# A Hymba decoder step: mixer norms on 32 partitions and as jobs between scan levels, sample states loaded two levels ahead, the last 264 tokens as two tiles of 128 and one of 8

## The chip, the core and the metric

The kernel runs on one NeuronCore of a Trainium2 chip. The metric is device time in microseconds (us), the median of several executions; lower is better. The core has five engines with their own instruction queues: PE (TensorE, matrix products), DVE (VectorE), ACT (ScalarE), POOL (GpSimd) and SP (SyncE, which here issues the DMAs).

## What is computed

One step of a hybrid decoder with one layer, in f32: 16 learned tokens and 1024 prompt tokens, which form one sequence, and 8 sample tokens, each with its own state; 1048 columns in all, model width 1024.

```python
h = h + 0.5 * swiglu(rmsnorm(h, n1), w1g, w1u, w1d)          # FFN 1, inner width 2816
u = rmsnorm(h, nm) @ w_in
q, fz, iv, g, z, xbc, dt_raw = jnp.split(u, SPLITS, axis=-1)
# HGRN2, 4 heads of 128: S_t = diag(f_t) S_{t-1} + k_t v_t^T, o_t = S_t^T q_t
o_hg = o_hg * lax.rsqrt(jnp.mean(o_hg * o_hg, axis=-1, keepdims=True) + EPS)   # per head
o_hg = o_hg.reshape(bsz, seqlen, HG_WIDTH) * hg_norm * jax.nn.silu(g)
# Mamba-2, 8 heads of 64, 2 groups, state 128, chunked scan; then
yz = (y * jax.nn.silu(z)).reshape(bsz, seqlen, SSM_GROUPS, -1)
yz = yz * lax.rsqrt(jnp.mean(yz * yz, axis=-1, keepdims=True) + EPS)           # per group of 256
h = h + jnp.concatenate([o_hg, yz], axis=-1) @ w_out
h = h + 0.5 * swiglu(rmsnorm(h, n2), w2g, w2u, w2d)          # FFN 2
y = rmsnorm(h, norm_final)
```

The prompt's results, the samples' results and the states of both kinds go out.

## The kernel before

Features lie on the 128 partitions and tokens along the free axis. Large products run at reduced operand precision with each operand split into a high and a low part, three matmuls for one (`mm3`, lines 163 to 165). The program has three stages: FFN 1, the mixer, and output projection with FFN 2 and the final norm.

In the FFNs the order on PE, DVE, ACT and SP is the program's own: a list of steps (`Steps`), each some matmuls of PE, with functions hung before a step by its number. In the mixer only PE's order is the program's; Tile's scheduler sets that of the other engines.

In the mixer the projections for q, f, v, g of each HGRN2 head and for z are a filler (`Fill`). One step of it, `fill(1)`, is one `mm3`, and `fill(n)` stands at every place where PE would wait for another engine. `fill.jobs` holds functions that run every so many fill steps; the Mamba-2 sample updates (`ssm_samples`) are such jobs.

The places the change touches:

- `ssm_scan`: nine chunks, eight of 128 tokens and one of 16. `back` makes the products with the old state (L1252), the causal block (L1257) and the new state (L1261).
- `hgrn_scan`: for each head a scan over levels m = 1, 2, 4, ... 64. A level has one batch of small products (L1540, or L1531 for m of 32 and more), then DVE multiplies q and k on (L1562, L1563), then `fill(5)`. `samples` loads four sample states and the samples' v rows, broadcast over the partitions, and updates them at once: four steps on ACT (L1488), four on DVE (L1489), then a store. It runs at m = 1 and m = 32. At the end the outputs are made in three pieces (L1619 to L1630); L1630 reads a sample's state with its q column, one column for each product.
- `hgrn_out` and `ssm_norm`: sums of squares over the partitions by a product with a matrix of ones (L1648, L1396), which puts the sum on all 128 partitions, then x to the power -1/2 by Ln, Exp and one Newton step (`rstd_wide`, L187) on 128 x 1032. `hgrn_out` returns five jobs, of which one runs after each level of the next head's scan; `ssm_norm` runs in one piece, that of group 0 ahead of head 1's scan.
- The final norm, on tokens: `Final` transposes 128 tokens (8 products), squares and sums on ACT, takes the root, and scales with `norm_final` on DVE. `LastFinal` does the last 264 of FFN 2's columns, three tiles of 88, in three parts, so that what is complete early is transposed early. They hang before steps of the last group of down products, whose results DVE adds to h (L763).

## Time and profile before

| | us |
|---|---|
| three executions | 1979.84, 1977.38, 1979.36 |
| median | 1979.36 |
| profiled execution | 1983.28 |
| its span | 1981.5 |
| PE busy in the span | 1937.6 |
| DVE, ACT, POOL busy | 1455.1, 835.4, 85.7 |

FFN 1 ends near 760 us, the mixer near 1190. A row of the windows view gives for a stretch of time its length, the busy time of the engines asked for (with instructions in brackets), the clock granted to TensorE as a share of full speed, the DMA engines' mean busy share and the GB/s moved. A row of the chain of waits gives start, length and work; a row of the timeline also shapes and, in square brackets, the idle time before it and what ended that. PEld is PE's weight loading.

### The profile page before, as it was taken

To read this page: it belongs to the slowest core of one execution; us is meant where nothing else is said; L and a number is where in the kernel's file an instruction comes from. 1 tells how busy PE (TensorE), PEld (TensorE's weight loads), DVE (VectorE), ACT (ScalarE), POOL (GpSimd) and SP (SyncE) were. 2 spreads that over 40 slices of the span, in tenths; PEclk is the share of its full clock that TensorE was granted. 3 is DMA by queue.
4 is the path that set the end of the run, shared out by engine and by line. 5 is a ranking of instruction groups with operands and counts; after the bars stand their busy time and mean duration, and the time that the engine had idled before them with its cause. 6 is when DMAs were issued, how large, how long until landed. Compare 5 with 4: busy or idle time off the path is not lost.

```text
span 1981.5 us, 40896 instructions
## 1 busy us (share of the span) xinstructions
PE 1937.6 (98%) x16687; PEld 1900.4 (96%) x16687; DVE 1455.1 (73%) x2515; ACT 835.4 (42%) x1587; POOL 85.7 (4%) x135
## 2 busy tenths in 40 slices
PE   7999999999999999999999999999999999999997
PEld 6999999999999999998989999999999999999997
DVE  7777777778688776575665567987777777768974
ACT  7522222224534655465544445742222222354352
POOL 4000000000000410000000002200000000000000
PEclk9999999999999999999999999999999999999999
DMA  7233242335976542232442254224232423487851
GB/s 219 78 100 98 82 129 82 112 83 155 295 246 223 175 133 60 55 102 63 131 121 67 78 167 141 71 87 117 85 109 81 127 83 113 152 245 237 270 179 67
DMA packets 323876, 258.45 MB, mean 130 GB/s; under 512 B 17568, under 2 KB 299424, under 8 KB 323680
## 3 DMA queue, kind: packets, MB, share of 16 engines
q1 hardware_dynamic: 323448, 255.79, 42.6%
q8 instruction: 132, 2.16, 0.5%
q14 instruction: 56, 0.46, 0.1%
q0 software_dynamic: 224, 0.04, 0.0%
q10 hardware_dynamic: 16, 0.00, 0.0%
HBM read 190.79 MB, written 65.05 MB: 129 GB/s over the span
## 4 chain that ended last, share of the span: by engine, by line
PE 84%; DVE 9%; DMA 2%; issue 2%; ACT 2%; SPq 0%; POOL 0%; DVEq 0%; ACTq 0%; POOLq 0%
PE acc L163 26%; PE acc L165 26%; PE acc L164 26%; DVE u L354 1%; DVE ws L468 1%; PE mis L1540 1%; DMA r<-in_w_ffn_up_dram 1%; DMA u<-hd 1%; DVE u L677 1%; DVE ws L739 1%; DVE u L343 0%; PE mis L1261 0%; DVE r L460 0%; PE mis L1600 0%; DVE t L548 0%
## 5 line engine op out<-in xcount | busy, mean ns | idle before, releaser
L163 PE MATMUL acc<-u,ws 128*128 128x258 f32 (+4 forms) x4482 | 1310.8, 293 | 8.4 <-DVE t L562 2.7
L164 PE MATMUL acc<-u,ws 128*128 128x258 f32 (+4 forms) x4482 | 1300.4, 290 | 3.3 <-DVE u L354 1.8
L165 PE MATMUL acc<-u,ws 128*128 128x258 f32 (+4 forms) x4482 | 1297.5, 290 | 3.4 <-DVE ws L468 3.3
L163 PEld LDWEIGHTS acc<-u,ws 128*128 128x128 f32 x4482 | 849.2, 190 | 13.6 <-issue 5.1
L164 PEld LDWEIGHTS acc<-u,ws 128*128 128x128 f32 x4482 | 851.6, 190 | 6.1 <-DVE u L354 2.8
L165 PEld LDWEIGHTS acc<-u,ws 128*128 128x128 f32 x4482 | 849.0, 189 | 5.3 <-DVE ws L468 4.9
L468 DVE TENSOR_TENSOR ws<-r,ws 128x512 fp32r<-128x512 f32 x308 | 212.8, 692 | 78.8 <-ACT ws L464 78.8
L464 ACT CAST ws<-r 128x512 fp32r<-128x512 f32 x308 | 173.8, 615 | 5.0 <-DVE r L460 4.8
L583 ACT ACTIVATE t<-t 128x524 f32<-128x524 f32 (+1 forms) x47 | 29.9, 640 | 299.6 <-DVE t L548 299.6
L460 DVE TENSOR_TENSOR r<-r,r 128x512 f32<-128x512 f32 x176 | 121.1, 690 | 8.3 <-DMA r<-in_w_ffn_up_dram 6.5
L560 ACT ACTIVATE t<-t 128x516 f32<-128x516 f32 (+1 forms) x41 | 26.2, 639 | 200.3 <-DVE t L548 200.3
L677 DVE TENSOR_TENSOR u<-u,u 128x1048 fp32r<-128x1048 f32 (+3 forms) x84 | 97.2, 1159 | 10.2 <-ACT u L673 9.4
L232 POOL TENSOR_TENSOR t<-t,t 128x262 f32<-128x262 f32 (+1 forms) x56 | 57.5, 1036 | 814.9 <-ACT t L231 811.8
L548 DVE TENSOR_TENSOR t<-t,u 128x524 f32<-128x524 f32 (+1 forms) x135 | 90.4, 698 | 2.8
L158 DVE TENSOR_TENSOR ws<-r,ws 128x512 fp32r<-128x512 f32 x88 | 60.9, 702 | 40.0 <-ACT ws L157 39.5
L734 ACT CAST ws<-u 128x512 fp32r<-128x512 f32 (+1 forms) x72 | 42.1, 585 | 99.9 <-DVE u L729 91.6
L673 ACT CAST u<-u 128x1048 fp32r<-128x1048 f32 (+3 forms) x84 | 82.8, 988 | 1.3 <-DMA u<-hd 1.3
L763 DVE SCALAR_TENSOR_TENSOR s<-acc,s 128x524 f32<-128x524 f32 (+3 forms) x86 | 53.8, 649 | 33.8 <-PE acc L165 33.5
L739 DVE TENSOR_TENSOR ws<-r,ws 128x512 fp32r<-128x512 f32 (+1 forms) x84 | 56.3, 681 | 29.8 <-ACT ws L734 29.5
L734 ACT CAST ws<-r 128x512 fp32r<-128x512 f32 (+1 forms) x84 | 47.5, 582 | 65.9 <-DVE r L729 39.7
L553 ACT COPY t<-acc 128x524 f32<-128x524 f32 (+3 forms) x46 | 26.4, 574 | 103.5 <-PE acc L165 103.5
L157 ACT CAST ws<-r 128x512 fp32r<-128x512 f32 x88 | 53.6, 617 | 34.5 <-PE acc L165 31.1
(393 smaller groups left out, 1875.2 us busy)
## 6 DMA issues: line engine op xcount, KB each, us to landing
r<-in_w_ffn_down_dram SPq DMA_DIRECT2D x128, 256.0 KB
hd<-s SPq DMA_DIRECT2D x93, 258.0 KB
r<-in_w_ffn_gate_dram SPq DMA_DIRECT2D x88, 256.0 KB
r<-in_w_ffn_up_dram SPq DMA_DIRECT2D x88, 256.0 KB
hd<-s SPq DMA_DIRECT2D x77, 262.0 KB
u<-hd SPq DMA_DIRECT2D x36, 516.0 KB
u<-hd SPq DMA_DIRECT2D x28, 524.0 KB
r<-in_w_in_dram SPq DMA_DIRECT2D x56, 256.0 KB
```

What stands on the lines that cost most here:

```text
L158: self.nc.vector.tensor_sub(lo, src, hi.bitcast(F32))
L163: mm(ps, whi, xhi, start=first, stop=False, skip_group_check=more)
L164: mm(ps, whi, xlo, start=False, stop=False, skip_group_check=more)
L165: mm(ps, wlo, xhi, start=False, stop=last, skip_group_check=more)
L460: self.K.nc.vector.tensor_tensor(self.raw[p], self.raw[x], self.raw[y], op)
L464: self.K.nc.scalar.copy(self.w[p][:, : self.n * P], self.raw[p])
L468: self.K.nc.vector.tensor_sub(t[:, 512 : 512 + w], self.raw[p], t[:, :w].bitcast(F32))
L548: nc.vector.tensor_mul(t, t if src is None else src, spread.lanes(i, cs))
L673: K.nc.scalar.copy(hi, lo.bitcast(F32))
L677: K.nc.vector.tensor_sub(lo, lo.bitcast(F32), hi.bitcast(F32))
L734: nc.scalar.copy(w[p, j, g][:, : n * P], src)
L739: nc.vector.tensor_sub(t[:, 512 : 512 + n * P], box[0], t[:, : n * P].bitcast(F32))
```

## The change

The norms of the mixer use a new class `Rms`. `root` makes four products whose weights are 32 columns of ones, so that the sums of the four quarters of the 1032 columns land on four strips of 32 partitions, 258 columns wide; Ln, Exp and (in `newton`, two jobs later) the Newton step run on that. `part(i)` spreads a quarter over 128 partitions by a product with one row of ones. `hgrn_out` multiplies the gate with the product's result in PSUM; `ssm_norm` copies it to SBUF, and returns seven jobs. Those of group 0 run after the levels of head 1's scan.

`samples` is parted: `samples_load` at m = 1 and m = 8, the update at m = 4 and m = 64. The samples' outputs are made from the other side: q column by q column padded to 32 columns of weights, the state as the moving operand, four results to a bank on strips of 32 partitions; the rows are copied and then turned by two transposes of four columns each.

In the 16-token chunk two `fill(2)` stand between the three products. `LastFinal` has tiles of 128, 128 and 8; a product of its first part goes from DVE to POOL, its squares of the second part become one instruction instead of two, and the three `Final` at the end stand at other steps, one with other banks.

```diff
+class Rms:
...
+    def root(self):
+        K, w = self.K, self.w
+        nc = K.nc
+        ps = K.psm()[:, :w]
+        for i in range(4):
+            nc.tensor.matmul(ps[32 * i : 32 * i + 32], K.ones[1][:, :32], self.v[:, i * w : i * w + w], start=True, stop=True)
+        self.r, self.q = K.t(w), K.t(w)
+        an = nc.scalar.activation(self.q, ps, AF.Identity, scale=self.scale, bias=K.eps)
+        with K.tc.issue_after(an.ins):
+            ld = nc.scalar.preload_act_table_set("natural_log_exp_and_others")
+        with K.tc.issue_after(ld.ins):
+            nc.scalar.activation(self.r, self.q, AF.Ln)
+            nc.scalar.activation(self.r, self.r, AF.Exp, scale=-0.5, bias=K.lna)
+    def newton(self):
...
+    def part(self, i):
+        K, w = self.K, self.w
+        ps = K.psm()[:, :w]
+        K.nc.tensor.matmul(ps, K.ones[1][32 * i : 32 * i + 1], self.r[32 * i : 32 * i + 1], start=True, stop=True)
+        return ps, slice(i * w, i * w + w)
...
+        if n < P:
+            fill(2)
         py = K.psm()
...
+        if n < P:
+            fill(2)
         ps = K.psm()
...
-def ssm_norm(K, g, tag, fill):
+def ssm_norm(K, g, tag, then):
...
+    return [rms.root, lambda: None, rms.newton, lambda: (spread(0), spread(1)), lambda: (spread(2), spread(3)), lambda: scale(0, ya), end]
...
-        if m in (1, 32):
-            samples({1: 0, 32: 4}[m])
+        if m in (1, 8):
+            samples_load({1: 0, 8: 4}[m])
         if jobs:
             jobs.pop(0)()
             fill(2)
+        if m in (4, 64):
+            samples({4: 0, 64: 4}[m])
         fill(5)
...
+    qz = K.t(32 * NS).rearrange("p (b i) -> p b i", b=NS)
+    nc.gpsimd.memset(qz, 0.0)
+    nc.scalar.copy(qz[:, :, 0], qs[:, :NS])
     fill(6)
+    pr = K.psm()
+    for b in range(NS):
+        nc.tensor.matmul(pr[32 * (b % 4) : 32 * (b % 4) + 32, b // 4 * P : b // 4 * P + P], qz[:, b], states[b // 4 * 4][:, b % 4], start=True, stop=True)
+    rows = K.t(2 * P)
+    nc.scalar.copy(rows, pr[:, : 2 * P])
+    fill(1)
...
-    for b in range(NS):
-        nc.tensor.matmul(po8[:, 16 + b : 17 + b], states[b // 4 * 4][:, b % 4], qs[:, b : b + 1], start=True, stop=True)
+    for i in range(2):
+        nc.tensor.matmul(po8[:, 16 + 4 * i : 20 + 4 * i], rows[:, i * P : i * P + P], K.ident[:, 0:P:32], start=True, stop=True)
...
-    jobs = [root, None, None, None, gate]
-    return [lambda i=i: jobs[i]() for i in range(5)]
+    return [rms.root, lambda: None, rms.newton, lambda: (gate(0), gate(1)), lambda: (gate(2), end())]
...
-            self.part(j, ps, 0, 4, 0)
+            K.nc.scalar.activation(yt[:n, 512:], ps[:n], AF.Square, accum_out=self.st[:n, 0, j : j + 1])
+            K.nc.scalar.copy(yt[:n, :512], ps[:n])
+            K.nc.gpsimd.tensor_mul(yt[:n, :512], yt[:n, :512], self.nf[0][:n, :512])
...
                 for fn in outs:
-                    fill(5)
+                    fill(4)
                     fn()
                 outs = []
                 fill.until("z0")
-                fill(10)
-                ssm_norm(K, 0, "s", fill)
-                for i in range(2):
-                    spill(2 + i, K.y[i][:, NM:])
+                fill(4)
+                outs = ssm_norm(K, 0, "s", lambda: [spill(2 + i, K.y[i][:, NM:]) for i in range(2)])
...
-        ssm_norm(K, 1, "s", fill)
+        fill(4)
+        for fn in ssm_norm(K, 1, "s", lambda: None):
+            fill(3)
+            fn()
...
-        for t0, at in ((3 * P, e3 + 6), (6 * P + 8, e3 + 11), (7 * P + 8, e3 + 16), (0, e0 + 1), (P, e0 + 3), (2 * P, e0 + 5)):
+        for t0, bank, at in (
...
+            (0, K.psm, (e0 + 1, e0 + 2, e0 + 3)),
+            (P, K.psum, (e0 + 2, e0 + 3, e0 + 4)),
+            (2 * P, K.psm, (e0 + 5, e0 + 6, e0 + 7)),
+        ):
...
-        last = LastFinal(K, o, h, nf, 4 * P, 88)
+        last = LastFinal(K, o, h, nf, 4 * P, 2 * P + 8)
```

How the instructions stand on the engines, at three places that the prediction speaks of (line, operation, output from inputs, size of the output; x8 means that eight alike follow one another).

PE, the 16-token chunk of the Mamba-2 scan, before. L163 to L165 are the filler; L1252, L1257 and L1261 the chunk's three products:

```order
L165 MATMUL acc_10609<-u_8341,ws_10346 128x344
L1252 MATMUL mis_10616<-u_9601,s_9725 128x16 x2
L1252 MATMUL mis_10616<-u_9707,s_9725 128x16 x2
L1257 MATMUL mis_10622<-s_10501,s_10511 64x16 x8
L1261 MATMUL mis_10631<-s_10511,s_10503 128x256 x2
L163 MATMUL acc_10609<-u_8342,ws_10346 128x344
```

The same place now, from the end of the first inserted `fill(2)` on (L1277 and L1283 are the second and the third product):

```order
L163 MATMUL acc_10609<-u_8343,ws_10346 128x344
L164 MATMUL acc_10609<-u_8351,ws_10346 128x344
L165 MATMUL acc_10609<-u_8343,ws_10346 128x344
L1277 MATMUL mis_10628<-s_10501,s_10511 64x16 x8
L163 MATMUL acc_10609<-u_8344,ws_10351 128x344
L164 MATMUL acc_10609<-u_8352,ws_10351 128x344
L165 MATMUL acc_10609<-u_8344,ws_10351 128x344
L163 MATMUL acc_10609<-u_8345,ws_10351 128x344
L164 MATMUL acc_10609<-u_8353,ws_10351 128x344
L165 MATMUL acc_10609<-u_8345,ws_10351 128x344
L1283 MATMUL mis_10643<-s_10511,s_10503 128x256 x2
L163 MATMUL acc_10609<-u_8346,ws_10351 128x344
```

The three products, which stood in a row, now have six filler matmuls between each two.

PE, the end of head 0's scan, before: the small third piece of the outputs, with the eight one-column reads of the sample states (L1630):

```order
L165 MATMUL acc_11350<-u_8342,ws_11070 128x344
L1626 MATMUL mis_11360<-p_1350_10796,vt_1342_10756 128x16
L1627 MATMUL mis_11360<-s_10798,s_11258 128x16
L1630 MATMUL mis_11360<-qs_10777,r_10879 128x1 x4
L1630 MATMUL mis_11360<-qs_10777,r_11171 128x1 x4
L163 MATMUL acc_11350<-u_8343,ws_11070 128x344
```

Now:

```order
L165 MATMUL acc_11355<-u_8343,ws_11079 128x344
L1668 MATMUL mis_11377<-p_1350_10796,vt_1342_10756 128x16
L1669 MATMUL mis_11377<-s_10798,s_11258 128x16
L1671 MATMUL mis_11377<-ident,t_11335 128x4 x2
L163 MATMUL acc_11355<-u_8344,ws_11079 128x344
```

Two transposes of four columns stand for the reads; the reads themselves, in the new form, stand ahead of the first two pieces.

DVE, near the end of the program, before. L763 adds a group of down products to h, L1736 scales the tiles of `LastFinal`, L1049 to L1053 are a root's Newton step and L1717 scales a tile of `Final`:

```order
L1736 TENSOR_TENSOR u_23406<-acc_23409,u_22639 88x512
L1736 TENSOR_TENSOR u_23407<-acc_23410,u_22639 88x512
L1736 TENSOR_TENSOR u_23408<-mis_23411,u_22639 88x512
L1049 RECIPROCAL ssq_23357<-ssq_23357 128x1
L1050 TENSOR_TENSOR ssq_23357<-ssq_23357 128x1
L1051 TENSOR_TENSOR ssq_23357<-ssq_23357 128x1
L1052 TENSOR_SCALAR ssq_23357<-ssq_23357 128x1
L1053 TENSOR_TENSOR ssq_23357<-ssq_23357 128x1
L1717 SCALAR_TENSOR_TENSOR u_23358<-mis_23359,ssq_23357,u_22639 128x512
L1717 SCALAR_TENSOR_TENSOR u_23358<-mis_23365,ssq_23357,u_22639 128x512
L763 SCALAR_TENSOR_TENSOR s_20985<-acc_23389,s_20985 128x258
```

Now (L1755 and L781 are the former L1717 and L763, L1798 scales in the second part of `LastFinal`):

```order
L1071 TENSOR_TENSOR ssq_23443<-ssq_23443 128x1
L1755 SCALAR_TENSOR_TENSOR u_23444<-mis_23445,ssq_23443,u_22717 128x512
L1755 SCALAR_TENSOR_TENSOR u_23444<-mis_23451,ssq_23443,u_22717 128x512
L781 SCALAR_TENSOR_TENSOR s_21063<-acc_23470,s_21063 128x258
L1798 TENSOR_TENSOR u_23495<-acc_23557,u_22717 128x256
```

The three products of 512 columns (L1736) are gone from DVE's queue ahead of the addition.

More of the change, by code (lines that the diff above doesn't have):

```diff
@@ L1391, in ssm_norm, with spread, scale, end @@
     nc.vector.tensor_add(v, v, r)
-    fill(10)
-    for c0, w in CHUNKS_O:
-        cs = slice(c0 - NM, c0 - NM + w)
-        ps = K.psm()[:, :w]
-        nc.tensor.matmul(ps, K.ones[1], v[:, cs], start=True, stop=True)
-        an = nc.scalar.activation(v[:, cs], ps, AF.Identity, scale=1.0 / 256, bias=K.eps)
-    for step in rstd_wide(K, v, r, an):
-        step()
-    for i, y in enumerate((ya, yb)):
+    rms = Rms(K, v, 1.0 / 256)
+    def spread(i):
+        ps, cs = rms.part(i)
+        nc.scalar.copy(r[:, cs], ps)
+    def scale(i, y):
         nc.vector.scalar_tensor_tensor(y, y, K.pc["ssm_norm"][:, 2 * g + i : 2 * g + i + 1], r, ALU.mult, ALU.mult)
+    def end():
+        scale(1, yb)
+        then()
+    return [rms.root, lambda: None, rms.newton, lambda: (spread(0), spread(1)), lambda: (spread(2), spread(3)), lambda: scale(0, ya), end]
 def hgrn_unit(K, a, hd, x, u, later=None):
@@ L1642, in hgrn_out, with gate, end @@
         nc.vector.scalar_tensor_tensor(g[:, cs], ps[:, :w], K.pc["hg_norm"][:, hd : hd + 1], g[:, cs], ALU.mult, ALU.mult)
[L1644 to L1653 removed]
+    rms = Rms(K, v, 1.0 / P)
+    def gate(i):
+        ps, cs = rms.part(i)
+        nc.vector.tensor_mul(g[:, cs], g[:, cs], ps)
+    def end():
+        gate(3)
         then()
[L1656 to L1657 removed]
+    return [rms.root, lambda: None, rms.newton, lambda: (gate(0), gate(1)), lambda: (gate(2), end())]
 def out_proj(K, a, h, part, ops, half, after=None):
```

105 lines of the change are left out of this document (47 added, 58 removed).

## Prediction

> **What bounds the kernel now.** I read the page's busy times first, then the long table of windows, then the waits of PE, and the chain and timeline only where those point.
>
> ```profile
> PE 1937.6 (98%) x16687; PEld 1900.4 (96%) x16687; DVE 1455.1 (73%) x2515; ACT 835.4 (42%) x1587; POOL 85.7 (4%) x135
> ...
> 900.00:1210.00 310.00, 302.83 (x3554) 0.97 0.36 105
> ```
>
> PE is the bound: 43.9 us of the span of 1981.5 without a matmul. The second row (windows of PE: length, busy, granted clock, DMA share, GB/s) is the stretch in which the mixer's scans run. PE is idle there for 310 - 302.83 = 7.2 us, and the clock stands at 0.97, so about 9 us more go in a stretch that looks busy. The next rows say where (windows of 10 us; the third number from the end is the clock):
>
> ```profile
> 910.00:920.00 10.00, 10.00 (x67) 8.98 (x68) 2.85 (x13) 3.08 (x5) 0.95 (x1) 0.83 0.10 27
> 940.00:950.00 10.00, 8.77 (x166) 8.22 (x166) 6.78 (x18) 3.88 (x11) 0.00 (x0) 0.83 0.51 140
> 970.00:980.00 10.00, 10.00 (x54) 8.83 (x53) 2.59 (x14) 4.27 (x13) 0.10 (x1) 0.83 0.59 176
> 980.00:990.00 10.00, 10.00 (x66) 10.00 (x65) 6.88 (x17) 8.61 (x18) 0.00 (x0) 1.00 0.17 52
> 1020.00:1030.00 10.00, 7.21 (x154) 6.77 (x154) 8.65 (x9) 5.54 (x10) 0.00 (x0) 0.70 0.31 99
> 1180.00:1190.00 10.00, 10.00 (x48) 7.78 (x47) 2.19 (x4) 4.47 (x9) 0.00 (x0) 0.83 0.91 320
> ```
>
> Four drops of 10 x 0.17 = 1.7 us and one of 3.0; the row of 980 is an undisturbed one, 66 matmuls at 0.15. In slices of 1 us (PE alone: busy, clock, DMA, GB/s) the first drop and the starts of three others are
>
> ```profile
> 911.00:912.00 1.00, 1.00 (x4) 0.71 0.00 0
> 914.00:915.00 1.00, 1.00 (x5) 0.58 0.00 0
> 942.00:943.00 1.00, 1.00 (x6) 0.57 1.11 262
> 972.00:973.00 1.00, 1.00 (x9) 0.93 0.01 4
> 1184.00:1185.00 1.00, 1.00 (x7) 0.74 0.91 297
> ```
>
> The clock halves at 911.42 and returns at 914.84: 3.42 us. The others start at 942.14, 972.86 and 1184.48, that is 30.72, 61.44 and 273.1 later: 9, 18 and 80 times 3.41. So the gate decides once per window of 3.41 us on a fixed grid. What stood in the windows ahead?
>
> ```profile
> 909.03 0.96 PE L1252 MATMUL mis<-u,s 128*128 128x16 f32 x8
> 909.92 0.64 PE L1257 MATMUL mis<-s,s 16*64 16x16 f32 x16
> 910.49 1.19 PE L1261 MATMUL mis<-s,s 16*128 16x256 f32 x4
> ...
> 970.97 1.77 PE mis L1630 x16
> ```
>
> Ahead of 911.42, the 16-token chunk of the state scan: small products from 909.0 on, 2.3 of 3.4 us. Ahead of 972.86, the sample reads of head 0: 16 instructions (an f32 product is two) that move one column each, 1.77 us. PE is "busy" in both, and the gate falls all the same. Ahead of 942.14 and of 1024.06 (33 windows after the first, inside the row of 1020) it stood still. The waits of PE in the mixer name that (total, times, longest):
>
> ```profile
> PE mis L1540 <- issue: 3.9, 4, 1.6
> PE mis L1512 <- ACT s L1466: 1.5, 1, 1.5
> PE mis L1540 <- DVE s L1501: 1.3, 1, 1.3
> PE acc L163 <- DVE s L1676: 0.5, 1, 0.5
> ```
>
> Rows two and three are one event, the norm of state-space group 0, whose wide steps stand ahead of head 1's first copies and products; in the chain (start, length):
>
> ```profile
> 1015.09 1.75 PE mis L1396 x6
> ...
> 1021.15 1.25 DVE s L203
> 1022.42 1.23 DVE s L204
> 1023.66 1.16 DVE s L1501
> ```
>
> **The change, part by part.** *Chunk of 16 tokens.* Two fill(2) part the three groups of small products. A fill step is 3 matmuls at 0.15, so each fill(2) is 0.9 us of dense work; the three groups with them span 4.1 us, and no 3.41 us can hold more than 1.6 us of small work (2.3 before). The drop goes: -1.7. The fill is only moved.
>
> *Sample reads of each head.* Out: 16 one-column instructions, 1.77 us (row L1630). In: eight products of 32 weight columns with 128 moving columns, to four strips of 32 output rows, then two transposes of 4 columns. The transposes are 4 instructions at 1.77/16 = 0.11: 0.45. For the strips the nearest row is
>
> ```profile
> 1021.19 0.77 PE L1511 MATMUL mis<-u,u 128*32 128x32 f32 x64
> ```
>
> also 32 weight columns into four strips: 64 instructions of 32 columns in 0.77 less a drain of about 0.2, 2048 columns, 0.28 ns a column. By row L1396, where nothing overlaps, 6 x 344 columns take 1.75: 0.85 ns. So 2048 columns cost 0.6 if strips overlap as in L1511, 1.74 if not. I take 0.6, as the strips are the same. Per head 1.77 - 1.05 = 0.7 saved (bounds: -0.4 to +0.9), four heads -2.9. The drops at 972.86 and 1184.52 go with the one-column work: -3.4. The new wait (transposes on the ACT copy of 256 columns) has four fill steps and 16 full products between, some 5 us; without them PE would wait for that copy, by L1565 below 0.4.
>
> *Norms on 32 partitions.* Before: 1032 columns at full width, 1.75 us, six times. After: four strip products of 258 columns, the L1511 form again, 0.6 (or 1.74), and four products with one row of weights that spread the root back, 258 columns each. No row has one-row products at four row places; by L1396 they cost 4 x 2 x 258 x 0.85 ns = 1.75, and half of that, 0.9, if the two of a pair overlap as strips do. I take 1.75, because the weights fill all columns as in L1396. Per norm 0.6 + 1.75 - 1.75 = +0.6; six norms +3.5 (bounds -1.5 and +10.4).
> The Trainium skill, "TensorE: Matmul & The Clock Gate", Part 3, says that products in different row strips run together and measures 3.07 times for four. No run here shows it; by it I estimate the pairs at 0.9 and the sum about 5 us lower.
> Three DVE steps and Ln, Exp now run on 258 columns instead of 1032:
>
> ```profile
> L1565 DVE TENSOR_TENSOR s<-s 128x260 f32<-128x260 f32 x4 | 1.7, 423 | 0.1
> L194 ACT ACT_TABLE_LOAD x6 | 7.7, 1283 | 0.1
> ```
>
> 0.42 against 1.23 (L204 above) a step. Off PE's path this costs nothing. ACT gains three table loads at 1.28, since a Silu now falls between Ln and Exp; the fill of a level, five steps or 2.3 us, covers each, and without cover that is 3.8 us.
>
> *Norm of group 0 as jobs in head 1's scan.* Its root no longer stands ahead of head 1's copies. The stall of 1.5 + 1.3 goes, and the drop behind it, 3.0, of which about 0.4 fell in idle time (half of the 0.8 from 1024.06 to the end of L1501): -2.8 and -2.6, together -5.4. Late next would be the scan's own products behind the norm's two Squares and their sum (1032 wide, by L204 about 1.2 each), with seven fill steps (3.2 us) a level over them instead of five.
>
> *Sample loads.* Both sets are loaded two levels before their use (for set 4, at level 8, used at 64), so ACT and DVE no longer stand in their queues for them. The DMAs stay the same; only the state load now goes ahead of weight loads in SP's queue. On PE the place shows as gaps inside L1540, 3.9 us in four, which the profile puts down to no wait ("issue"); they stand where DMA is busy (262 GB/s in the row of 942). Whether moved loads free them I can't say: half, -1.95, and half of the drop at 942.14, -0.85. Sum -2.8 (bounds 0 and -5.6).
>
> *Hand-over to the output projection.* DVE has six steps of 0.42 instead of 1.23 there: the 0.5 behind L1676 goes. Against it, PE now has four one-row products and a strip root in a row, 2.3 us of weak work, as long as the chunk's: half a drop, +0.9. Sum +0.4.
>
> *The last 264 tokens.* Timeline of PE and DVE at the end:
>
> ```profile
> 1961.71 0.28 PE L165 MATMUL acc<-u,u 128*128 128x258 f32 x1
> 1963.14 0.28 PE L165 MATMUL acc<-u,u 128*128 128x258 f32 x1
> 1965.02 0.86 PE L1729 MATMUL acc<-ident,s 128*88 128x128 f32 x6 [1.60 <-DVE s L763]
> ...
> 1968.43 0.28 PE L165 MATMUL acc<-u,u 128*128 128x258 f32 x1
> 1970.49 0.42 PE L1729 MATMUL acc<-ident,s 128*88 128x128 f32 x2 [1.78 <-DVE s L763]
> ...
> 1950.92 0.43 DVE L763 SCALAR_TENSOR_TENSOR s<-acc,s 128x258 f32<-128x258 f32 x1 [4.40 <-PE acc L165]
> ...
> 1962.26 0.15 DVE L1049 RECIPROCAL ssq<-ssq 128x1 f32<-128x1 f32 x1
> ...
> 1963.22 1.41 DVE L1717 SCALAR_TENSOR_TENSOR u<-mis,ssq,u 128x512 f32<-128x512 f32 x2
> 1964.55 0.42 DVE L763 SCALAR_TENSOR_TENSOR s<-acc,s 128x258 f32<-128x258 f32 x1
> ```
>
> PE waits 1.6 and 1.8 us because DVE makes the last additions (L763) only after the norms of finished tiles: the group that ends at 1961.71 is added at 1964.55. Afterwards three DVE products of the first half go to POOL, and finished tiles end a step or two sooner. From the addition at 1950.92 (0.9 later, as a tile's eight transposes now stand ahead of it) DVE has three tiles at 0.96 + 1.41 (from L1049 to the end of L1717), two roots with their trip to ACT at about 0.6 and two additions: 9.2 us, to 1961.0, ahead of 1961.71. Both waits shrink to the bare addition: -3.2 (at worst 0, at best -3.4). POOL's three products of 512, at twice the 1.04 of
>
> ```profile
> L232 POOL TENSOR_TENSOR t<-t,t 128x262 f32<-128x262 f32 (+1 forms) x56 | 57.5, 1036 | 814.9 <-ACT t L231 811.8
> ```
>
> take 6.2 us; they begin with the first copy, ahead of 1961.71, so they end by 1967.9, before the last group's addition and the scaling that reads them. Without that cover each costs 2.1. Three tiles of full-width steps stay three, and as many bytes are stored: nothing after the last product.
>
> **Sum.** -1.7 - 2.9 - 3.4 + 3.5 - 5.4 - 2.8 + 0.4 - 3.2 = -15.5 us. The profiled execution took 1983.28 (span 1981.5), so 1967.8, a ratio of 0.9922; on the median of 1979.36 that is **1964 us**.
>
> **Rivals.** (A) *The gate falls as often.* The windows lie on a grid, and which small stretch fills one depends on the phase: L1630 ran in four heads and cost a drop in two. Strip and one-row products may be as weak as one-column ones. If new drops replace the old, the gain loses 1.7 + 3.4 + 2.6 + 0.85 less the 0.9 set aside at the hand-over, 7.65: -7.9, 1972. For it: 2.3 us of small work sufficed. Against: the new groups are mostly 0.6 to 1.7 us between fills of 2.3 and more. The Trainium skill, same page, Part 1, lets the clock halve after an idle window of about 3.4 us; the rows show the same length, but PE had matmuls all through the window ahead of 911.42, so here the trace does not agree on the condition. By that rule the drops at 911, 972 and 1184 have another cause and would stay, 5.1 us: an estimate of 1969.
> (B) *The stalls only move.* ACT and DVE stand in a new order throughout the mixer, with more table loads. If head 1 waits as long elsewhere and the gate follows (5.4), the loads free nothing (2.8) and the strips don't overlap (6.9), -15.5 becomes -0.4: 1979, no change. For it: DVE is busy 8.65 of 10 us at 1020. Against: two thirds of the norm's width goes from there.
> (C) *Strip and one-row products count as idle for the gate.* Six roots and 12 pairs of spreading products; six pairs and three roots stand beside a level's batch of
>
> ```profile
> L1540 PE MATMUL mis<-s,u 128*32 128x16 f32 x1280 | 15.8, 187 | 5.7 <-issue 3.9 <-DVE s L1501 1.3 <-DVE u L1563 0.3
> ```
>
> (20 batches, 0.8 us each), so 1.4 to 2.5 us weak, and the rest at the hand-over or between fills. Each place that halves a window costs 1.7; from ten of the 18 on the change loses, and at twelve it is -15.5 + 20.4: 1984. Against: the L1540 batches themselves, 32 columns wide, halve no window unless PE also stops.
>
> **Numbers.** The forecast 0.66, A 0.17, B 0.09, C 0.08. Within 0.2% (4 us, about what a measurement of this kernel can tell) lie most of B and a little of A: faster 0.83, same 0.09, slower 0.08. The forecast's own bounds (norms +6.9 and -5, loads +2.8 and -2.8, reads +4.5 and -0.7, not all at once) give 1955 to 1973; with A and part of B the range is 1955 to 1976.
>
> **What would show it.** In the profile of the changed kernel: clock 1.00 through 905 to 920 and after each head's sample reads; no PE wait on the first copies of head 1; the pair of spreading products near 0.9 us (0.45 if they overlap), the root near 0.6 plus drain; no wait of PE over 0.5 at the last two sets of transposes, and the last addition near 3 us earlier against the end of PE's work. I'm wrong if the clock rows show as many halves as before, or if the spreading products stand with waits on DVE in front.

## The result, and the profile after

The changed kernel takes 1959.53 us (median of 4 executions, 1958.27 to 1961.39) against 1979.6 for the kernel before, measured beside it, 20 us less; the ratio of the executions is 0.9906, 95% interval 0.9893 to 0.9919, that is 16 to 21 us. The forecast of 1964 was 4.5 us too high. The profiled execution took 1961.39 us, 21.9 less than the one of before.

The page of the changed kernel (busy times), then its windows of all engines (length, busy time and count of PE, PEld, DVE, ACT and POOL, then clock, DMA share and GB/s):

```profile
PE 1924.7 (98%) x16763; PEld 1885.4 (96%) x16763; DVE 1441.9 (74%) x2523; ACT 830.4 (42%) x1580; POOL 90.1 (5%) x144
```

```profile
900.00:1190.00 290.00, 287.51 (x3603) 267.45 (x3602) 174.09 (x461) 152.86 (x315) 7.09 (x17) 1.00 0.38 113
910.00:920.00 10.00, 10.00 (x76) 8.62 (x76) 1.99 (x9) 2.52 (x4) 0.96 (x1) 1.00 0.09 26
970.00:980.00 10.00, 9.57 (x64) 8.22 (x64) 6.38 (x29) 8.14 (x17) 0.00 (x0) 1.00 0.36 103
1000.00:1010.00 10.00, 10.00 (x195) 9.26 (x194) 7.47 (x17) 5.75 (x10) 0.00 (x0) 1.00 0.13 29
1170.00:1180.00 10.00, 9.52 (x86) 8.11 (x80) 6.48 (x12) 7.33 (x15) 0.00 (x0) 1.00 0.63 225
```

The stretch of the scans is now some 18 us shorter (chunk to hand-over in the table below), PE is idle in it for 2.5 us instead of 7.2, and its clock is 1.00 instead of 0.97: all five drops are gone. It is hardly the luck of one execution: the mean granted clock was 0.997 in all four executions of the changed kernel, and 0.989 to 0.995 in all 41 of the kernel before that ran beside the experiments. A window of 3.41 us at half clock lowers that mean by 0.0009, so in the three executions without a profile it leaves room for one drop in the mixer, perhaps two. It can't say more, because drops outside the mixer, in the first 45 us of nearly every profile, enter the same mean.

The waits of PE that are left in the parts that the change touches (total, times, longest):

```profile
PE mis L1570 <- issue: 1.4, 1, 1.4
PE acc L1769 <- DVE s L781: 0.6, 1, 0.6
PE mis L223 <- DVE t L217: 0.4, 1, 0.4
PE mis L203 <- ACT s L1418: 0.4, 1, 0.4
```

L1570 is the scan's batch (L1540 before), with 3.9 in four; no wait stands on head 1's first copies; the 3.4 at the last transposes have become 0.6. The new products in the timeline of PE: reads and their transposes, a root, a pair of spreading products, and eight spreading instructions at the hand-over.

```profile
959.63 0.64 PE L1650 MATMUL mis<-r,t 128*32 128x128 f32 x16
...
967.62 0.59 PE L1671 MATMUL mis<-ident,t 128*128 128x4 f32 x4
...
970.13 0.64 PE L203 MATMUL mis<-s,ones 128*32 128x258 f32 x8
...
979.79 0.70 PE L223 MATMUL mis<-t,ones 1*128 1x258 f32 x4
...
1175.45 0.72 PE L223 MATMUL mis<-t,ones 1*128 1x258 f32 x8
```

The length of a row holds a drain; the next fill product begins 0.57, 0.45, 0.58 and 0.64 us after the start of the first four. Eight one-row instructions take hardly longer than four.

**Where the time went.** The same instruction was looked up in both timelines, at places with the same number of fill products ahead, so that the difference of two times is what the stage between them gained:

| stage of the profiled execution, us | before | after | difference | the prediction's terms for it |
|---|---|---|---|---|
| start to the chunk of 16 tokens | 909.03 | 909.23 | +0.2 | 0 |
| to the first transpose of v in head 0 | 15.43 | 14.22 | -1.2 | -1.7 |
| to head 0's state products (its levels) | 34.31 | 30.87 | -3.4 | -2.2 |
| to head 3's state products | 210.64 | 200.65 | -10.0 | -7.5 |
| to the norm behind the output projection's first half | 68.69 | 65.56 | -3.1 | -0.8 |
| to the transposes of the first tokens' tile | 709.24 | 709.98 | +0.7 | 0 |
| to the last transposes | 23.15 | 20.09 | -3.1 | -3.2 |
| to the end of the span | 11.01 | 9.10 | -1.9 | 0 |

The seven lines from the chunk on are what the experiments are compared by as well. The first line is not: in the 14 profiles of this study the chunk begins between 907.8 and 912.7 us, though nothing ahead of it was changed. A part of that spread is the clock as well: six of the 14 profiles have a drop near 766 us, at the start of the mixer, and reach the chunk at 909.6 to 912.7; the eight without, before and after among them, reach it at 907.8 to 909.6. That spread, and the 1 to 2 us by which the stage of FFN 2 differs, is why a median can lie a few us off what its stages say.

### The profile page after: what moved, and what is told of

Same layout as the page of the kernel before. It is cut to its first block, busy times and chain, and to the rows that moved or that the text cites. A ratio compares the mean times of both kernels' runs of the same rounds, so it can differ in the third digit from the quotient of the medians.

```text
span 1959.7 us, 41077 instructions
## 1 busy us (share of the span) xinstructions
PE 1924.7 (98%) x16763; PEld 1885.4 (96%) x16763; DVE 1441.9 (74%) x2523; ACT 830.4 (42%) x1580; POOL 90.1 (5%) x144
## 4 chain that ended last, share of the span: by engine, by line
PE 85%; DVE 8%; DMA 2%; ACT 2%; issue 2%; SPq 0%; POOL 0%; DVEq 0%; ACTq 0%; POOLq 0%
PE acc L163 26%; PE acc L165 26%; PE acc L164 26%; DVE u L372 1%; PE mis L1570 1%; DVE ws L486 1%; DMA u<-hd 1%; DVE u L695 1%; DVE u L361 1%; PE mis L1283 0%; DVE r L478 0%; DVE t L566 0%; DMA r<-in_w_ffn_down_dram 0%; DVE ws L757 0%; PE mis L1632 0%
## 5 line engine op out<-in xcount | busy, mean ns | idle before, releaser
L163 PE MATMUL acc<-u,ws 128*128 128x258 f32 (+4 forms) x4482 | 1308.4, 292 | 7.9 <-DVE t L580 2.2
L165 PE MATMUL acc<-u,ws 128*128 128x258 f32 (+4 forms) x4482 | 1295.3, 289 | 3.5 <-DVE ws L486 3.5
L163 PEld LDWEIGHTS acc<-u,ws 128*128 128x128 f32 x4482 | 846.6, 189 | 18.5 <-issue 10.2
L165 PEld LDWEIGHTS acc<-u,ws 128*128 128x128 f32 x4482 | 846.5, 189 | 5.3 <-DVE ws L486 4.9
L482 ACT CAST ws<-r 128x512 fp32r<-128x512 f32 x308 | 173.8, 615 | 4.9 <-DVE r L478 4.8
L601 ACT ACTIVATE t<-t 128x524 f32<-128x524 f32 (+1 forms) x47 | 29.9, 640 | 298.9 <-DVE t L566 298.9
L781 DVE SCALAR_TENSOR_TENSOR s<-acc,s 128x524 f32<-128x524 f32 (+3 forms) x86 | 53.8, 649 | 29.9 <-PE acc L165 29.6
L757 DVE TENSOR_TENSOR ws<-u,ws 128x512 fp32r<-128x512 f32 (+1 forms) x72 | 47.4, 659 | 26.5 <-ACT ws L752 26.5
```

The lines of the kernel that those rows point to most:

```text
L163: mm(ps, whi, xhi, start=first, stop=False, skip_group_check=more)
L165: mm(ps, wlo, xhi, start=False, stop=last, skip_group_check=more)
L482: self.K.nc.scalar.copy(self.w[p][:, : self.n * P], self.raw[p])
L757: nc.vector.tensor_sub(t[:, 512 : 512 + n * P], box[0], t[:, : n * P].bitcast(F32))
```

## The experiments

All but before_parted are the changed kernel with one edit. Times are medians of 4 to 12 executions in five rounds, weak_stretches apart; ratios are against the kernel before, run beside them.

### What lowers the clock

*weak_stretches* adds work ahead of each head's copy of the sample reads; it leaves nothing out.

```diff
+    if hd == 0:
+        for _ in range(16):
+            for b in range(NS):
+                nc.tensor.matmul(pr[32 * (b % 4) : 32 * (b % 4) + 32, b // 4 * P : b // 4 * P + P], qz[:, b], states[b // 4 * 4][:, b % 4], start=True, stop=True)
+    if hd == 1:
+        for _ in range(36):
+            nc.tensor.matmul(pr[:, 256:384], K.ones[1][:1], K.ones[1][:1], start=True, stop=True)
+    if hd > 1:
+        for _ in range(8 if hd == 2 else 6):
+            for b in range(2 if hd == 2 else 5):
+                nc.tensor.matmul(pr[:, 256 + b : 257 + b], states[b // 4 * 4][:, b % 4], qs[:, b : b + 1], start=True, stop=True)
+            fill(1)
```

> The changed kernel with work added ahead of each head's copy of the sample reads, to see what the gate counts; the added products write scratch or write the same values again. Head 0: the eight strip products of the reads 16 times more, about 8 us. Head 1: 36 products with one row of weights, 128 columns, about 8 us. Head 2: eight times two one-column products and a fill step. Head 3: six times five one-column products and a fill step. Measured by what the array does in a window of 3.41 us (rows x columns of weights x columns moved, against a window of fill products), the profiles so far have a drop behind all windows below 0.34, none behind windows above 0.41. By that theory: head 0 near 0.48, clock 1.00; head 1 near 0.03, the clock halves from the second window on; head 2 near 0.47, clock 1.00; head 3 near 0.29, the clock halves. Rival 1 (only an idle PE lowers the clock): 1.00 in all four. Rival 2 (C of the prediction: small products count as idle whatever they do): drops in heads 0, 1 and 3, and in head 2 where half the time is small. The time itself is about 30 us over the changed kernel's, since the added work is not hidden.

One execution, 1997.31 us, 38 over the changed kernel where 30 were set. Timeline of PE in the four stretches, then windows of 1 us inside each (length, PE busy, clock, DMA share, GB/s):

```profile
957.29 1.27 PE L1654 MATMUL mis<-r,t 128*32 128x128 f32 x40
...
1053.83 5.56 PE L1657 MATMUL mis<-ones 1*128 1x128 f32 x34
...
1121.53 0.50 PE L1661 MATMUL mis<-qs,r 128*128 128x1 f32 x4
...
1182.40 1.28 PE L1661 MATMUL mis<-qs,r 128*128 128x1 f32 x10
```

```profile
961.00:962.00 1.00, 1.00 (x47) 1.00 0.00 0
1054.00:1055.00 1.00, 1.00 (x11) 1.00 0.00 0
1057.00:1058.00 1.00, 1.00 (x7) 0.50 0.00 0
1121.00:1122.00 1.00, 1.00 (x9) 1.00 0.25 99
1188.00:1189.00 1.00, 1.00 (x6) 0.50 0.00 0
```

PE is busy in every one of them. Strips keep the clock (heads 0 and, mixed with fill, 2); one-row products lose it from 1055.9 for three windows, the thin mix of head 3 from 1185.6 for five. Rivals 1 and 2 of this run are out. To put a number on it, I added up over each 3.41 us of a profile's grid, for all matmuls of its timeline, rows x columns of weights x columns moved, and divided by what the FFN's products of 258 columns, one every 0.12 us, would do. The windows of the four stretches have 0.54 to 0.65, 0.00, 0.56 to 0.61 and 0.27. (I had set 0.48 and 0.47 for the strips and head 2: strips overlap better, and the breaks cost less.) In the stretch of the scans and the start of FFN 2 (about 905 to 1320 us), over 13 profiles (all but the changed kernel's own) and without the windows that follow a drop directly:

| work in the window, columns of weights counted | windows | clock halved in the next |
|---|---|---|
| 0.00 to 0.32 | 15 | 14 |
| 0.34 to 0.403 | 6 | 5 |
| 0.411 and above | 1514 | 0 |

The rest of the program shows that this is not yet what the gate counts. From 755.3 to 763.0 us the mixer makes 48 products with only 16 columns of weights (the projection for dt). Rows of the changed kernel, a matmul and a window:

```profile
758.11 0.32 PE L1096 MATMUL acc<-u,wdt 128*16 128x350 f32 x1
...
758.00:760.00 2.00, 2.00 (x14) 1.00 0.01 2
```

By the sum above their windows have 0.09 to 0.16, less than nearly every window that halved the clock, and in all 14 profiles not one of these 28 windows halved it. Without the columns of weights, as rows x columns moved, they have 0.60 to 1.02, and the count fits the whole program. All 14 profiles, from 15 us to 1945 us, windows at full clock (in the first 15 us, 18 windows of 0.28 to 0.38 had no drop behind them; why stays open):

| work in the window, rows x columns moved | windows | clock halved in the next |
|---|---|---|
| 0.00 to 0.38 | 41 | 41 |
| 0.38 to 0.44 | 19 | 5 |
| 0.44 and above | 7798 | 0 |

So an idle PE is one case of it, not the condition: 19 of the 46 drops follow a window in which PE was busy throughout. The clock halves after a window in which the array took in less than about 0.4 of a dense window's rows x columns moved; where the border lies between 0.38 and 0.44 these profiles do not settle, and that it is this product and not another count that goes with it is a fit to these kernels. Strips count in full by it, and four run at a time: those of head 0 have 2.2. For products with all columns of weights, as the chunk's first and third and the one-column reads, the two sums are the same; where they differ below, the text says so. When the clock returns is open too: a halved window of 0.29 was followed by a full one, one of 0.33 by another halved one.

*chunk_unparted* takes the two fill(2) out of the chunk.

```diff
-        if n < P:
-            fill(2)
         py = K.psm()
...
-        if n < P:
-            fill(2)
         ps = K.psm()
```

> The changed kernel (1959.5 us) without the two fill(2) inside the chunk of 16 tokens; the three groups of small products stand together again. Theory (2.3 us of small products in a row halve the clock for one window of 3.41 us): a row near 910 us with clock 0.83, and the part from the first product of that chunk to the first transposes of head 0, which went from 15.43 us in the kernel before to 14.22 in the changed one, is back near 15.4: about 1960.7. Rival 1 (the drop needed the phase of one execution): clock 1.00 there, and since two breaks in the dense work fall away, some 0.5 us faster than the changed kernel: 1959.0. Rival 2 (the drop has a cause outside the chunk): no difference, 1959.5, and the clock as in the changed kernel.

1963.46 us (1959.12 to 1965.67), 0.9912 (0.9900 to 0.9925). In its profile the clock stays at 1.00 there and the stage takes 13.95 us, 0.27 less than the changed kernel: rival 1 for this execution. Its grid cut the small products so that their window did 0.45; sliding the window over the timeline, 0.39 of all phases would put one below 0.352, and 0.57 below 0.43, two borders on either side of the range in doubt. The mean clocks of the five executions, 0.995 to 0.997, say that some had a drop more, but not where, and drops near 766 us and in the first 45 us come and go too. So where the chunk's drop fell, in the kernel before, the stage took 15.43 us against 13.95; by the phases it falls in part of the executions only, and parting costs 0.27: the term is worth under 1.2 on average, not 1.7, and an estimate from the phases gives 0.3 to 0.6. The median does not tell.

*before_parted* is the kernel before with nothing but fill steps moved.

```diff
+        if n < P:
+            fill(2)
         py = K.psm()
...
+        if n < P:
+            fill(2)
         ps = K.psm()
...
     for b in range(NS):
+        if b == 4:
+            fill(2)
         nc.tensor.matmul(po8[:, 16 + b : 17 + b], states[b // 4 * 4][:, b % 4], qs[:, b : b + 1], start=True, stop=True)
```

> The kernel before with nothing but fill steps moved: two fill(2) between the three groups of the chunk of 16 tokens, and one fill(2) in the middle of each head's eight one-column reads. No work is taken away. Theory (a window of 3.41 us in which the array does less than about a third of a dense window's work halves the clock in the next): no drop at the chunk and at the four reads, which fell in 0.7, 0.7, 0.4, 0.4 and 0.4 of the phases, so 2.6 drops of 1.5 us go and six breaks of about 0.2 come: 1979.6 - 3.9 + 1.2 = 1976.9, with drops left only at the stall of head 1 and where a gap stands. Rival (only an idle window lowers the clock; the breaks are pure loss): 1980.8 and as many drops as before.

1977.43 us, 0.9985 (0.9975 to 0.9995): faster by 3.0 us (1.0 to 4.9) with the same work, which a rule of idle windows can't give. The chunk and the reads of heads 0 and 3 show no drop in its profile; those of heads 1 and 2 still do, behind windows of 0.40 and 0.36. Two fill steps between the halves were not quite enough.

### The sample reads

*reads_by_column* puts the one-column reads back, without the strips, the copy of the rows and its fill(1).

```diff
-    for b in range(NS):
-        nc.tensor.matmul(pr[32 * (b % 4) : 32 * (b % 4) + 32, b // 4 * P : b // 4 * P + P], qz[:, b], states[b // 4 * 4][:, b % 4], start=True, stop=True)
-    rows = K.t(2 * P)
-    nc.scalar.copy(rows, pr[:, : 2 * P])
-    fill(1)
+    for b in range(NS):
+        nc.tensor.matmul(po8[:, 16 + b : 17 + b], states[b // 4 * 4][:, b % 4], qs[:, b : b + 1], start=True, stop=True)
```

> The changed kernel with the sample reads of each head as before: eight products with one moving column each, no strips and no transposes. Theory (one-column products are slow and halve the clock): 1.79 against 0.58 + 0.45 us in four heads, 3.0 us, and a drop of 1.7 us in those heads whose reads fill a window of the grid, two of four as in the kernel before: 1959.5 + 3.0 + 3.4 = 1965.9. Rival (A of the prediction: the drops come from the phase and not from the reads): clock 1.00 after all four, 1962.5. If the reads cost no PE time that matters: 1959.5.

1975.93 us (1969.28 to 1981.89), 0.9983 (0.9971 to 0.9995): 16 us dearer, and no theory had more than 6.4. In its profile 13.8 of them lie between the chunk and the hand-over. All four reads have a drop behind them, and there is a stall that nobody expected. Timeline of ACT, and the wait of PE that follows:

```profile
970.68 1.28 ACT L208 ACT_TABLE_LOAD   x1
971.97 0.42 ACT L210 ACTIVATE t<-t 128x258 f32<-128x258 f32 x1
972.41 1.28 ACT L1443 ACT_TABLE_LOAD   x1
973.70 0.46 ACT L1443 ACTIVATE u<-acc 128x344 f32<-128x344 f32 x1
974.18 1.28 ACT L211 ACT_TABLE_LOAD   x1
975.47 0.51 ACT L211 ACTIVATE t<-t,lna 128x258 f32<-128x258 f32 x1
```

```profile
979.16 0.90 PE L223 MATMUL mis<-t,ones 1*128 1x258 f32 x4 [3.21 <-DVE t L217]
```

One fill step less ahead of the norm, and the Silu of a gate's evacuation (L1443) falls between Ln (L210) and Exp (L211) of head 0's root, with a table load on each side. Exp begins 3.1 us after the end of Ln, and PE waits 3.2 us for the root, with a fifth drop (from 979.55) behind the idle window. The Newton steps on DVE take as long as in the changed kernel (3.0 and 3.1 us). There the same Silu stands ahead of the root, and the wait is 0.4.

*reads_by_column_in_step* differs from it by one number.

```diff
-    fill(6)
+    fill(7)
```

> The changed kernel with one-column sample reads, as in the run reads_by_column, but with one fill step more ahead of them, so that every later fill step stands where it does in the changed kernel. In reads_by_column a Silu of the gate's evacuation came between Ln and Exp of head 0's norm, its two table loads made Exp late, and PE waited 3.2 us for the root, with a drop behind it. Theory (that stall hangs on where the fill steps stand, not on the reads): no such wait; the reads cost 1.34 us more in PE in each of four heads less the strips' 0.75 and their break, 3.0 in all, and the windows at the reads fall below a third of a window's work in 0.4 to 0.7 of the phases of the grid, 2.3 drops of 1.5 us: 1959.5 + 3.0 + 3.4 = 1966. Rival 1 (the stall belongs to the reads): it is there again, near 1971 to 1976. Rival 2 (no drops at these reads): 1962.5.

1971.53 us, 0.9955 (0.9943 to 0.9968). The stall is gone (its wait on L217 is 0.4, and Silu stands ahead of the root again), so it hangs on the phase of the fill steps and not on the reads: rival 1 is out. From the chunk to the hand-over its profile takes 317.19 us against 311.30, 5.9 more, with two drops, which is the theory's 6.4. But the median is 12 us above the changed kernel's. The two profiled executions differ by 10.1: besides the 5.9, 3.5 lie ahead of the chunk (912.73 against 909.23), where this profile has three drops and the changed kernel's one, and 0.6 in FFN 2. The remaining 1.9 is the changed kernel's profiled execution, which lies that much above its own median.

### The norms

*spread_full_rows* makes the products of a pair use all rows of the array, with the same result.

```diff
-        K.nc.tensor.matmul(ps, K.ones[1][32 * i : 32 * i + 1], self.r[32 * i : 32 * i + 1], start=True, stop=True)
+        K.nc.tensor.matmul(ps, K.ident[:, 32 * i : 32 * i + 1].broadcast_to([P, P]), self.r, start=True, stop=True)
```

> The changed kernel with the root spread back by products of 128 rows of weights (a column of the identity, repeated), so that the two products of a pair no longer stand on different rows of the array; the numbers they make are the same. Theory (the one-row products run together, which is why a pair took 0.64 us of PE where 0.88 and the breaks were set): eight pairs 0.4 us dearer, 3.5, and the two groups of eight instructions at the hand-over 1.2 each, 2.4: 1959.5 + 5.9 = 1965.4, and a pair near 1.08 us in the profile. Rival 1 (a pair is bound by its breaks and weight loads, not by whether its products overlap): 1959.5. Rival 2 (the work of a pair decides, and full rows are faster than one row): below 1959.

1962.85 us, 0.9919 (0.9905 to 0.9932). Timeline of PE, the rows that answer to 979.79 and 1175.45 above:

```profile
980.41 1.03 PE L223 MATMUL mis<-t,ident 128*128 128x258 f32 x4
...
1177.46 1.98 PE L223 MATMUL mis<-t,ident 128*128 128x258 f32 x8
```

Eight instructions take 1.98 us on full rows and 0.72 on four different rows of the array; a pair 1.03 and 0.70. That the one-row products run together is shown, for one row alone is not faster: the 36 of weak_stretches, all on the same row, took 0.112 us for each instruction of 128 columns, 0.87 ns a column, about what L1648 of before takes on full rows (1.82 us for 2064 columns, 0.88 ns). The price of full rows is smaller than I set: chunk to hand-over 2.1 us more, and 1.2 of gap (below) less, so 3.3, as the medians have it, not 5.9; beside fill, part of a pair's length hides in its breaks.

*norm0_whole* brings back only the norm of state-space group 0 at full width, in one piece ahead of head 1's scan (ssm_norm_wide is the old ssm_norm, with rstd_wide).

```diff
-                fill(4)
-                outs = ssm_norm(K, 0, "s", lambda: [spill(2 + i, K.y[i][:, NM:]) for i in range(2)])
+                fill(10)
+                ssm_norm_wide(K, 0, "s", fill)
+                for i in range(2):
+                    spill(2 + i, K.y[i][:, NM:])
```

> The changed kernel with the norm of state-space group 0 in one piece at full width ahead of head 1's scan, as in the kernel before; all other norms stay on 32 partitions. Theory (stall and drop of head 1): the waits of 1.5 and 1.3 us on head 1's first copies and products come back, and behind them a drop of the clock of 1.7 to 3.0; the root itself is cheaper in one piece (1.47 us against 0.56 + 0.63 + 0.64): 1959.5 + 2.8 + 2.6 - 0.4 = 1964.5. Rival 1 (the stall returns, but the gate does not fall at another phase of its grid): 1961.9. Rival 2 (B of the prediction: the stall had only moved to another place in head 1): 1959.5.

1968.57 us, 0.9945 (0.9932 to 0.9958). Its waits of PE in the mixer, and the clock behind them (windows of PE):

```profile
PE mis L1584 <- ACT s L1534: 1.5, 1, 1.5
PE mis L1612 <- DVE s L1573: 1.3, 1, 1.3
PE acc L163 <- issue: 0.9, 1, 0.9
PE mis L1624 <- DVE p L1627: 0.6, 1, 0.6
```

```profile
1010.00:1020.00 10.00, 7.98 (x109) 1.00 0.01 2
1020.00:1030.00 10.00, 8.33 (x175) 0.83 0.63 195
```

Both old waits are back on the same instructions (L1512 and L1540 of before), with a drop of 1.7 behind a window of 0.04 (0.15 without the columns of weights), and smaller waits after them. From head 0's state products to head 1's it takes 94.88 us against 87.50; six fill products more stand in it (0.95), so the norm's place and width are worth 6.4, against 5.4 set. Rival B is out. The median shows 9.0; of the profile, 2.8 lie ahead of the chunk, with four drops there against one.

*norm0_narrow_ahead* keeps the narrow norm, but ahead of the scan.

```diff
-                outs = ssm_norm(K, 0, "s", lambda: [spill(2 + i, K.y[i][:, NM:]) for i in range(2)])
+                for fn in ssm_norm(K, 0, "s", lambda: [spill(2 + i, K.y[i][:, NM:]) for i in range(2)]):
+                    fill(3)
+                    fn()
```

> The changed kernel with the norm of state-space group 0 on 32 partitions, but again ahead of head 1's scan, its seven jobs three fill steps apart, instead of inside the scan's levels. It tells the width of the norm's steps from their place. Theory 1 (the narrow steps alone free ACT and DVE for head 1's first copies): no wait over 0.4 on them, 1959 to 1960. Theory 2 (the place decides: two Squares, the wide sum and the two wide scalings still stand ahead of head 1's copies): waits of 1 to 3 us, with a drop behind them: 1961 to 1964.5.

1963.81 us, 0.9917 (0.9904 to 0.9931), 3.8 us dearer from chunk to hand-over. Both theories miss half. No wait stands on head 1's first copies, so the narrow steps alone free ACT and DVE for them. But the root itself now waits for the 1032 wide sum of squares, and a drop follows (from 1004.97):

```profile
PE mis L203 <- DVE s L1413: 1.9, 1, 1.9
```

As jobs inside the levels, the first level's fill and products cover that sum.

### The sample loads

*loads_as_before* loads and updates at levels 1 and 32.

```diff
-        if m in (1, 8):
-            samples_load({1: 0, 8: 4}[m])
+        if m in (1, 32):
+            samples_load({1: 0, 32: 4}[m])
+            samples({1: 0, 32: 4}[m])
...
-        if m in (4, 64):
-            samples({4: 0, 64: 4}[m])
```

*loads_ahead_of_levels* loads the first set ahead of the levels and the second at level 1.

```diff
+    samples_load(0)
     fill(3)
...
-        if m in (1, 8):
-            samples_load({1: 0, 8: 4}[m])
+        if m == 1:
+            samples_load(4)
```

> The changed kernel with the sample loads as before: load and update together at levels 1 and 32. Theory (the queues stand for the loads, and the gaps inside the scan's batches come from it): the gaps without a releaser inside the batches, 3.9 us in four before and 1.4 in one after, are back, with the drop of 1.7 us at the second of them: 1959.5 + 2.5 + 1.7 = 1963.7. Rival 1 (the gaps have nothing to do with the loads and the drop went because the grid lies otherwise): 1959.5 with gaps as in the changed kernel. Between them, the half that the prediction took: 1962.3.

> The changed kernel with both sample loads still earlier: the first set ahead of the levels, the second at level 1. Theory 1 (the gaps without a releaser inside the scan's batches come from the sample loads beside them): no gap over 0.3 us in head 0's levels, and these take 29.4 us from the transposes of v to the state products, as in the runs without a gap, where the changed kernel took 30.9: 1958.0. Theory 2 (the gaps come from any burst of DMA, the weight loads too, and stand where the batch happens to meet one): still one or two gaps of 0.3 to 1.8 us, now elsewhere: 1959 to 1961. If the earlier loads collide with the loads of the weights: a wait on a split weight, over 1961.

1960.50 us, 0.9902 (0.9889 to 0.9915), and 1960.90 us, 0.9903 (0.9890 to 0.9917): neither differs from the changed kernel. Head 0's levels take 31.70, 30.87 (the changed kernel) and 29.48 us, with these gaps in their batches:

```profile
939.49 0.47 PE L1570 MATMUL mis<-s,u 128*32 128x16 f32 x35 [1.52 <-issue]
```

```profile
932.10 0.18 PE L1570 MATMUL mis<-s,u 128*32 128x16 f32 x1 [1.42 <-issue]
```

and none. That looks like theory 1, but tail_as_before, tail_88_rows and spread_full_rows run the changed kernel's instructions up to that place, and have gaps of 0.5, 0.3 and none in the whole mixer, with 29.7 to 29.9 us for these levels. So a gap of 0 to 1.5 us comes and goes with the execution. The old place may invite them (in all 3.9, 3.1 and 1.8 us in the three profiles of the old order), but reads_by_column has 2.8 with the new one. What PE waits for in a gap stays open: the long ones stand where the DMA share is 0.4 to 1.1, two short ones where it is 0.04 and 0.16.

### The last 264 tokens

*tail_as_before* has the old Final and LastFinal and their old places (the diff of the change, backwards). *tail_88_rows* keeps the new steps and changes the shape alone.

```diff
-        self.tiles = [(t0 + c, min(P, n - c)) for c in range(0, n, P)]
+        self.tiles = [(t0 + c, 88) for c in range(0, n, 88)]
```

> The changed kernel with the last tiles and the last 264 tokens as before (three tiles of 88 rows, the old order of their steps). Theory by the traces: the two waits of PE come back, 3.0 us, and the last store, 88 rows instead of 8, ends 1.9 later after the last step of DVE: 1959.5 + 4.9 = 1964.4. Rival 1 (the prediction's own term, the waits alone): 1962.7. Rival 2 (the waits were hidden by something that is late anyway): 1959.5.

> The changed kernel, all new steps of the tail kept, but the last 264 tokens again as three tiles of 88 rows. Theory (the shape of the last tile sets only the last store): PE's waits as in the changed kernel, 0.6 us in one, and from the last step of DVE to the end of the span 6.4 us instead of 4.4: 1959.5 + 1.9 = 1961.4. Rival 1 (the 1.9 us come from the order of the new steps and not from the size of the last store): 1959.5 with 4.4 us after the last step. Rival 2 (whole tiles also free PE, because their steps begin on time): waits of 1 to 3 us are back, 1962 to 1964.

1964.32 us, 0.9929 (0.9915 to 0.9942), and 1961.12 us, 0.9911 (0.9898 to 0.9925). The last two stages: 23.16 and 10.96 us with the old tail, 20.07 and 11.08 with the new steps on 88 rows, 20.09 and 9.10 in the changed kernel. The two parts come apart cleanly: the order of the steps is worth 3.1, the shape 2.0. Timelines of SP's last three stores, of tail_88_rows and of the changed kernel:

```profile
1951.85 2.38 SPq L1722 DMA_DIRECT2D out_dram<-u  x3
```

```profile
1953.93 1.72 SPq L1722 DMA_DIRECT2D out_dram<-u  x3
```

The last store now carries 8 rows: SP issues the three in 0.66 us less, and the span ends 4.0 us after the last issue instead of 5.4.

## Why the prediction was right, point by point

- **PE's bound and the drops: right.** All five drops went in the profiled execution, and the clocks of the other three agree. (The drop at 1024 is two windows, 3.4 us; the 3.0 of the prediction are what its row of 10 us shows of it.) The reason was right as well, that small products and not only idle time halve the clock; weak_stretches and before_parted show it. But smallness itself is not it: what goes with the drops is rows x columns moved. Strips and products with 16 columns of weights, as small, keep the clock; products of one moving column or one row lose it. Rival C falls with that for the strips, and its one-row pairs, which are as weak as it feared, stand in windows with enough fill. The Trainium skill, "TensorE: Matmul & The Clock Gate", Part 1, ties the halving to an idle window of about 3.4 us; the length agrees (3.41), the condition does not (windows with 0.27 of the work and PE busy throughout halved the clock).
- **Chunk, -1.7: measured -1.2** in one pair of executions, less on average by the phases, since the parting costs 0.27 in all. I had taken the drop of one execution for all. The profiled execution of the kernel before had that drop and the phase decides it, so the full -1.2 is in part luck.
- **Sample reads, -2.9 and -3.4: right in kind.** The strips took 0.57 and the transposes 0.45, as set. On PE's path the strips cost 0.2 more, the break in the fill (from head 0's state products to its 16-token piece 12.73 us against 11.48 in reads_by_column, with three fill products, 0.47, more). Two drops were a fair number, and partly luck: sliding the window over the timeline of before, the four reads fall below 0.352 in 0.7 and three times 0.4 of the phases, 1.9 in all (2.9 with the border at 0.43), and not always the same ones; reads_by_column had all four, the run in step two.
- **Norms on PE, +3.5: the term that was mis-sized.** I took 1.75 us for the four spreading products, "because the weights fill all columns as in L1396". They run on different rows of the array and overlap: two pairs take 1.28 with their breaks, eight instructions at the hand-over 0.65. A norm beside the scan costs PE what it did before (0.58 + 1.28 against 1.82 from 976.60 to the next fill), and the two at the hand-over take 0.58 + 0.65 = 1.23 instead of 1.75: -1.0 in all, inside the lower bound of -1.5. That is 4.5 us. The Trainium skill's Part 3 of the same page, by which I had estimated 5 us less, was the better price: 1.98 against 0.72 us is 2.75 times for eight instructions with their drain.
- **Norm 0 as jobs, -5.4: 6.4** by norm0_whole; the stall and the drop were where the prediction put them, and smaller waits behind them came on top. norm0_narrow_ahead shows that width and place each do a part.
- **Sample loads, -2.8: not shown.** Head 0's levels gained 3.4, but undoing the loads gave back 0.8 in the profile and nothing that the medians can tell. The step "whether moved loads free them I can't say: half" took the gaps for a matter of the loads; they vary with the execution.
- **Hand-over, +0.4: about -0.1.** The wait of 0.5 went, one of 0.4 on the last root's statistics came, and the half drop that I set aside for 2.3 us of weak work did not: the poorest window there does 0.47, or 0.69 by rows x columns moved, because the overlap makes the products short and strips are not weak.
- **Last 264 tokens, -3.2: 3.1**, as worked out. But "as many bytes are stored: nothing after the last product" failed: all stores but the last are hidden, and only the last one's size shows, 2.0.

By the table, the 6.3 us between the sum of -15.5 and the 21.8 of the two spans are 4.8 in the two stages with the norms (the norms' 4.5, norm 0's 1.0 and the hand-over's 0.5 more, against breaks that the strips and jobs add), 1.2 in head 0's levels (gaps and a drop that vary) and 1.9 at the last store, less 1.5 from the chunk and from stages that the change hardly touches.

## What to carry to other kernels

Before a thin product goes between dense ones, add up rows x columns moved in the poorest 3.4 us around it; here a window below about 0.4 of a dense one cost 1.5 us afterwards, and two dense steps moved between thin ones, in six places, bought 3.0 us back with no work removed. Where no drop would have fallen, the two breaks of the chunk cost 0.27. A small product is cheap when it shares the array with others in other strips, and dear when it moves one column through all of it. And after the last product, the size of the last store is time: put the small remainder last.

## What was not expected of the hardware

- The halving of the clock goes with rows x columns moved, not with busy time, and not with the columns of weights: 36 one-row products in a row, PE busy throughout, halved the clock for three windows; 7 us of 32-column strips, and 8 us of products with 16 columns of weights, did not.
- One-row products on four different rows of the array took 0.72 us for eight instructions of 258 columns, 1.98 on full rows.
- With two table loads of 1.28 us between Ln and Exp of one norm, PE waited 3.2 us instead of 0.4, and one fill step decided whether they came.
- Kernels that are the same ahead of the mixer reach its 16-token chunk up to 4.9 us apart: between 907.8 and 912.7 us in 14 profiles, the later ones mostly with a drop near 766 us.
